# A fourth group of four feature blocks by seven products in the down projection, and the final norm's table loaded in the second half

## The chip, the core and the metric

The kernel runs on one core of one Trainium2 chip. The time is the device time of one execution in microseconds; the kernel before took 1541.56 us (median of 3 runs, 1541.18 to 1541.80).

## What is computed

One layer of a decoder trunk on x of 1 x 256 x 2048 float32: two token mixers, a gated feed-forward part with a causal convolution, and a last RMSNorm. The change touches the last projection of the feed-forward part and the norm behind it:

```python
    h = rmsnorm(x, norm_ffn_w[l])
    gate, up = jnp.split(jnp.einsum('bsd,df->bsf', h, w_up[l]), 2, axis=-1)
    gate = causal_dwconv(gate, conv_ffn_w[l]) + conv_ffn_b[l]
    x = x + jnp.einsum('bsf,fd->bsd', jax.nn.gelu(gate, approximate=False) * up, w_down[l])
return rmsnorm(x, norm_final_w)
```

Here S = 256 tokens, D = 2048 and d_ff = 5632, so w_down is 5632 x 2048.

## The kernel before

**Numbers in two parts.** A float32 operand is kept as two float32r parts: a high part (whi, hhi), made by a cast on ACT (L289), and a low part (wlo, hlo), the difference, made by a subtraction on DVE (L297; called a split below). A product of two operands is three matmuls: high by high, low by high, high by low (`products`, L1356). One matmul takes 128 features of 128 tokens against 128 x 512 of a weight.

**Down projection.** The features are 11 chunks of four blocks of 128 (chunk c: `hhi[c]`, `hlo[c]`); the columns are worked in two halves of 1024, each two tiles of 512. A weight tile is 256 features x 512 columns (0.52 MB). A plain step takes one weight tile against both token halves: 2 x 2 x 3 = 12 matmuls. Four plain steps do a chunk in one column half.

**Seven products.** For the chunks in `SEVEN` a column half is done by Strassen's method in Winograd's form: h of the chunk is a 2 x 2 matrix (token half by feature half), the weights are one (feature half by column tile: parts "11", "12", "21", "22"), and instead of eight products of parts there are seven, of 6 matmuls each (`PRODUCTS`, L152). Products "11", "21" and "T4" take h itself; "T1", "T2", "T3" and "22" take sums of h, which `half_sums` (L1292) makes once a chunk: an addition that puts h together, four sums of 128 x 256 (L1281 to L1284), a cast and a split. On the weights' side T1, T3, T2 and T4 are differences of parts, which DVE forms in place ahead of the cast (L283, tile names quad). The seven results are put together at the end of a half by additions into u and by `plus` (L1573 to L1581, L1504).

**Order.** `stream` (L158) writes the order of the weights of a half: `gaps` gives how many plain steps stand ahead of each group of seven, and behind each product but the first stands one more plain step. With `keeps`, behind the plain steps of the given numbers a weight for the very end is loaded and split early (khi, klo). `begin` (L276) casts and splits two weights ahead of PE's; whi and wlo have three buffers each, the raw loads four. SP issues the raw loads (L209). The 24 parts of the six groups are loaded by POOL's queue (`next_quarter`, L237) into eight places that are handed round (`HOMES`); one is asked for behind each cast of a T product. A scheduler then places the instructions of each engine, in the order that the notation of the fences below shows.

**Around it.** xt and xtl are the residual's tiles (L1555), `weighted` (L1510) multiplies one of their 128 x 512 blocks by the final norm's table nfin, which one transfer of 1 MB on ACT's queue loads ahead of the down projection (L1488) into tile x0. The second half ends with four streamed and four kept weights (`ends`).

Of the kernel before, what the change touches and what calls it, by code (L numbers as in the profile page):

```python
# [35 lines left out]
def kernel(  # L36
# [196 lines left out]
    HOMES = (("xt0", "xt1", "xt2", "xt3"), ("x1a", "x1b", "x2a", "x2b"), ("xt2", "xt3", "x1b", "x1a"),  # L233
             ("x2a", "x2b", "xt3", "xt2"), ("x1b", "x1a", "x2b", "x2a"), ("xt3", "xt2", "x1a", "x1b"))
    asked = [(g, i) for g in range(6) for i in range(4)]

    def next_quarter():  # L237

        if asked:
            g, i = asked.pop(0)  # L240
            half, chunk, what, home = g // 3, SEVEN[g % 3], ORDER[i], HOMES[g][i]
            r = (fp if home[:2] == "xt" else big).tile([P, 2, 512], F32, tag=home, name=nm("quad"))
            nc.gpsimd.dma_start(r, down[2 * half + int(what[1]) - 1][2 * chunk + int(what[0]) - 1])
            quarters[half, chunk, what] = r
# [1047 lines left out]
    def half_sums(c):  # L1292

        if c == SEVEN[2]:
# [152 lines left out]
    for i, step in enumerate(up_steps):  # L1447
# [13 lines left out]
        elif step[0] == "plain":  # L1461
# [6 lines left out]
            if step[1] == NUP - 1 and step[2] == 0:  # L1468
                if step[3] == 5:
                    with tc.issue_after(last_split[0]):  # L1470
                        half_sums(SEVEN[0])
# [15 lines left out]
    nfin = big.tile([P, D], F32, tag="x0", name="nfin")  # L1487
    nc.scalar.dma_start(nfin, norm_final_w.partition_broadcast(P))  # L1488
# [21 lines left out]
    def weighted(t, c):  # L1510
        nc.vector.tensor_tensor(block(t, c), block(t, c), nfin[:, c * 512 : (c + 1) * 512], op=ALU.mult)
# [7 lines left out]
    for hf in range(2):  # L1519
# [11 lines left out]
        for n, step in enumerate(steps[hf]):  # L1531
# [19 lines left out]
            if what == "11" and chunk == SEVEN[1 + hf]:  # L1551
# [4 lines left out]
            if hf == 0 and what == "T2" and chunk != SEVEN[-1]:  # L1556
                with tc.issue_after(last_split[0]):
                    half_sums(SEVEN[SEVEN.index(chunk) + 1])
# [8 lines left out]
            products(ps, high, low, w, alone and what not in began, alone and chunk == SEVEN[-1])  # L1567
            began.add(what)
            if chunk == SEVEN[-1] and what == PRODUCTS[-1]:
# [27 lines left out]
    for t in range(2):  # L1597
        ts = slice(t, t + 1)

        def scaled(c, by, queue):  # L1600
# [5 lines left out]
            else:  # L1606
                nc.vector.scalar_tensor_tensor(xs, xs, rs[:, ts], nfin[:, c * 512 : (c + 1) * 512],
# [70 lines left out]
```

## Time and profile before

| | |
|---|---|
| runs, us | 1541.56 (1541.18 to 1541.80) |
| profiled execution, us | 1542.63 |
| its span, first to last instruction, us | 1540.8 |
| PE busy in the span | 1526.0 us, 99% |
| DVE busy | 1253.4 us, 81% |
| ACT busy | 849.8 us, 55% |
| DMA moved | 310.46 MB, 201 GB/s on average |
| first half of the down projection | about 1299 to 1414 us |
| second half | 1414 to 1533 us; its last split ends at 1516 |

The busy share is an average over stages. In timeline rows the first number is the start in us from the span's start, the second how long the row's instructions took, then engine, line, operation and tiles (written <- read); the last part in brackets is the idle time before it and who ended it. Instructions on PE and DVE overlap at their ends, so what counts for the pace is the distance from start to start, not the length.

### The profile page before, as it was taken

The page shows a single profiled execution, that of the slowest core. Times are in us where ns is not written, and L with a number is a line of the kernel's source. Part 1 is how long each engine was busy: PE and PEld are TensorE (multiplying, and loading weights), DVE is VectorE, ACT ScalarE, POOL GpSimd, SP SyncE. Part 2 cuts the span into 40 slices and gives each one's busy share as a digit, 9 for nine tenths or more (in the row PEclk, how much of TensorE's full clock was granted, in tenths as well). Part 3 has the DMA queues.
Part 4 walks back from the last instruction along what each step waited for, and adds up shares of the span by engine and source line. Part 5 has one row for each costly group of instructions (what it writes and reads, how often), then busy time and mean ns, then how long its engine had stood idle before and what let it go on. Part 6 is the DMA issues. An engine that isn't in the chain of part 4 may idle for free.

```text
span 1540.8 us, 20209 instructions
## 1 busy us (share of the span) xinstructions
PE 1526.0 (99%) x7302; PEld 1257.4 (82%) x7302; DVE 1253.4 (81%) x1776; ACT 849.8 (55%) x1063; POOL 70.8 (5%) x90
## 2 busy tenths in 40 slices
PE   9999999999999999999999999999999999999998
PEld 8887888788878888788888888888788888888886
DVE  6788859896589858987667899999999886878885
ACT  7455446454455445454455676666667665555552
POOL 1010002000100000000000000000000000000100
PEclk9999999999999999999999999999999999999999
DMA  8776757776577766776578646666457467556652
GB/s 276 215 221 199 202 163 214 213 214 183 152 245 205 205 169 201 222 200 186 179 250 300 194 163 217 219 205 205 150 155 242 125 216 267 183 193 205 227 189 90
DMA packets 166674, 310.46 MB, mean 201 GB/s; under 512 B 19458, under 2 KB 23330, under 8 KB 166446
## 3 DMA queue, kind: packets, MB, share of 16 engines
q1 hardware_dynamic: 159456, 287.37, 60.0%
q0 software_dynamic: 5184, 18.88, 3.7%
q10 hardware_dynamic: 1934, 2.93, 0.5%
q8 instruction: 57, 0.93, 0.2%
q14 instruction: 43, 0.35, 0.1%
HBM read 301.75 MB, written 7.38 MB: 201 GB/s over the span
## 4 chain that ended last, share of the span: by engine, by line
PE 92%; DVE 4%; issue 2%; DMA 1%; ACT 0%; POOL 0%; POOLq 0%; DVEq 0%; ACTq 0%
PE psg L1374 25%; PE psm L334 15%; PE psm L332 14%; PE psm L333 14%; PE psm L1359 7%; PE psg L1359 7%; DVE wlo L297 3%; PE psm L1374 2%; PE psm L478 1%; PE psg L377 1%; DVE quad L230 1%; PE psm L1436 1%; DMA vrow<-ev 1%; PE psg L868 1%; DMA mv<-vrow 1%
## 5 line engine op out<-in xcount | busy, mean ns | idle before, releaser
L289 ACT CAST whi<-raw 128x1024 fp32r<-128x1024 f32 x428 | 450.0, 1052 | 428.4 <-PE psm L333 280.2
L297 DVE TENSOR_TENSOR wlo<-raw,whi 128x1024 fp32r<-128x1024 f32 x426 | 517.3, 1220 | 151.2 <-ACT whi L289 146.2
L289 ACT CAST whi<-quad 128x1024 fp32r<-128x1024 f32 x168 | 176.1, 1054 | 141.0 <-DVE quad L230 39.4
L297 DVE TENSOR_TENSOR wlo<-quad,whi 128x1024 fp32r<-128x1024 f32 x168 | 202.6, 1219 | 36.2 <-ACT whi L289 35.3
L334 PE MATMUL psm<-wlo,xhl 128*128 128x512 f32 x432 | 169.5, 393 | 1.6 <-DVE wlo L297 1.6
L332 PE MATMUL psm<-whi,xhl 128*128 128x512 f32 x432 | 169.0, 391 | 0.0
L333 PE MATMUL psm<-whi,xhl 128*128 128x512 f32 x432 | 168.6, 390 | 0.0
L1374 PE MATMUL psg<-whi,fhl 128*128 128x512 f32 x504 | 127.1, 389 | 0.0
L1374 PEld LDWEIGHTS psg<-whi,fhl 128*128 128x128 f32 x504 | 94.4, 188 | 19.5
L334 PEld LDWEIGHTS psm<-wlo,xhl 128*128 128x128 f32 x432 | 81.1, 188 | 19.0 <-DVE wlo L297 2.4
L333 PEld LDWEIGHTS psm<-whi,xhl 128*128 128x128 f32 x432 | 81.1, 188 | 16.8
L332 PEld LDWEIGHTS psm<-whi,xhl 128*128 128x128 f32 x432 | 81.1, 188 | 16.6
L230 DVE TENSOR_TENSOR quad<-quad,quad 128x1024 f32<-128x1024 f32 x72 | 87.6, 1217 | 0.0
L1374 PE MATMUL psg<-wlo,fhl 128*128 128x512 f32 x252 | 69.9, 389 | 0.0
L1374 PE MATMUL psg<-whi,ups 128*128 128x512 f32 x216 | 58.9, 394 | 0.0
L1359 PE MATMUL psm<-whi,hhi 128*128 128x512 f32 (+1 forms) x150 | 58.1, 387 | 0.0
L1359 PE MATMUL psm<-whi,hlo 128*128 128x512 f32 (+1 forms) x150 | 57.9, 386 | 0.0
L1359 PE MATMUL psm<-wlo,hhi 128*128 128x512 f32 (+1 forms) x150 | 57.4, 387 | 0.1
L1374 PEld LDWEIGHTS psg<-wlo,fhl 128*128 128x128 f32 x252 | 47.3, 188 | 9.8
L332 PE MATMUL psm<-whi,mhi 128*128 128x512 f32 x128 | 50.8, 397 | 0.0
L1359 PE MATMUL psg<-whi,hhi 128*128 128x512 f32 (+1 forms) x130 | 50.3, 387 | 0.4 <-ACT whi L289 0.4
L1359 PE MATMUL psg<-whi,hlo 128*128 128x512 f32 (+1 forms) x130 | 50.0, 386 | 0.0
(432 smaller groups left out, 2927.3 us busy)
## 6 DMA issues: line engine op xcount, KB each, us to landing
raw<-in_w_in_dram SPq DMA_DIRECT2D x224, 512.0 KB, 4.2
raw<-in_w_up_dram SPq DMA_DIRECT2D x104, 512.0 KB, 4.8
quad<-in_w_up_dram SPq DMA_DIRECT2D x72, 512.0 KB, 4.9
raw<-in_w_down_dram SPq DMA_DIRECT2D x64, 512.0 KB, 4.7
raw<-in_w_out_dram SPq DMA_DIRECT2D x32, 512.0 KB, 4.2
quad<-in_w_down_dram POOLq DMA_DIRECT2D x24, 512.0 KB, 5.5
mv<-vrow SPq DMA_DIRECT2D x12, 512.0 KB, 4.9
taps<-in_conv_qkv_w_dram SPq DMA_DIRECT2D x16, 256.0 KB, 6.8
```

Of the source, the lines that this page charges most:

```text
L230: nc.vector.tensor_tensor(out_, plus_, minus_, op=ALU.subtract)
L289: nc.scalar.copy(hi, raw)
L297: last_split[0] = nc.vector.tensor_tensor(lo, raw, hi.bitcast(F32), op=ALU.subtract).ins
L332: mm(ps[:, t, :], lh(k, t), hi[:, kk, :], start=(k == 0), stop=False)
L333: mm(ps[:, t, :], ll(k, t), hi[:, kk, :], start=False, stop=False)
L334: mm(ps[:, t, :], lh(k, t), lo[:, kk, :], start=False, stop=(k == nk - 1))
L377: nc.tensor.transpose(pt[:, ff, t * P : (t + 1) * P], src[:, t, f * P : (f + 1) * P], ident)
L478: mm(ps_k0[:, t, :], part(k, t), w[:, kk, :], start=(k == 0 and w is hi and part is xh), stop=(k == KD - 1 and w is lo))
L868: mm(pg0, kq[:, h, 0, 0:P], kq[:, h, :, :], start=True, stop=True)
L1359: mm(ps[:, cs], lhs(kk), part_[:, kk, cs], start=(first and kk == 0 and n == 0), stop=(last and kk == 1 and n == 2), skip_group_check=shared)
L1374: mm(ps, lhs(kk), w[n][:, kk], start=(first and n == 0 and kk == 0 and lhs is high), stop=False, skip_group_check=True)
L1436: nc.tensor.transpose(out_[f // 2][:, f % 2, t * P : (t + 1) * P], e[:, t, f * P : (f + 1) * P], ident)
```

## The change

Chunk 7 joins chunks 8, 9 and 10: in the first half as the fourth group, in the second as the first. A product is now followed by a plain step only behind T1, T3, T2 and "21". The gaps and the keeps change with it. The parts' eight places are handed round by a rule that gives the six old rows and two more. `half_sums` gets places for chunk 7 (tiles y and x0). The norm's table is loaded by POOL's queue in the second half, at product "22" of its second group, into x0, and the four `weighted` of the first half's blocks move from the turn of the halves to product "22" of the last group.

```diff
-    SEVEN = (8, 9, 10)
+    SEVEN = ((8, 9, 10, 7), (7, 8, 9, 10))
     PRODUCTS = ("11", "T1", "22", "T3", "T2", "21", "T4")
-    DIRECT = [c for c in range(KF // 4) if c not in SEVEN]
+    DIRECT = [c for c in range(KF // 4) if c not in SEVEN[0]]
...
-        for n, chunk in zip(gaps, SEVEN):
+        for n, chunk in zip(gaps, SEVEN[half]):
             plain(n)
             for i, what in enumerate(PRODUCTS):
                 steps[half].append(("part", chunk, what))
                 srcs.append((half, chunk, what))
-                if i:
+                if i in (1, 3, 4, 5):
                     plain(1)
         plain(len(todo))
...
-    stream(0, DIRECT, (6, 3, 3))
-    stream(1, DIRECT[:-2], (3, 1, 1), (9, 13, 17, 21))
+    stream(0, DIRECT, (5, 2, 2, 1))
+    stream(1, DIRECT[:-2], (3, 1, 0, 0), (8, 12, 16, 20))
...
-    HOMES = (("xt0", "xt1", "xt2", "xt3"), ("x1a", "x1b", "x2a", "x2b"), ("xt2", "xt3", "x1b", "x1a"),
-             ("x2a", "x2b", "xt3", "xt2"), ("x1b", "x1a", "x2b", "x2a"), ("xt3", "xt2", "x1a", "x1b"))
-    asked = [(g, i) for g in range(6) for i in range(4)]
+    homes = [("xt0", "xt1", "xt2", "xt3"), ("x1a", "x1b", "x2a", "x2b")]
+    while len(homes) < 8:
+        homes.append((homes[-2][2], homes[-2][3], homes[-1][1], homes[-1][0]))
+    asked = [(g, i) for g in range(8) for i in range(4)]
...
-            h = fp.tile([P, 4, S], F32, tag="hlo10" if c == SEVEN[0] else "eu", name=nm("whole"))
+            h = fp.tile([P, 4, S], F32, tag={8: "hlo10", 9: "eu", 7: "y"}[c], name=nm("whole"))
             nc.vector.tensor_tensor(h, hhi[c].bitcast(F32), hlo[c].bitcast(F32), op=ALU.add)
-            b = fp.tile([P, 2, 4, S], F32R, tag="ups", name="sx") if c == SEVEN[0] else \
-                big.tile([P, 2, 4, S], F32R, tag="x3", name="sx")
+            b = fp.tile([P, 2, 4, S], F32R, tag="ups", name="sx") if c == 8 else \
+                big.tile([P, 2, 4, S], F32R, tag="x3" if c == 9 else "x0", name="sx")
...
-    nfin = big.tile([P, D], F32, tag="x0", name="nfin")
-    nc.scalar.dma_start(nfin, norm_final_w.partition_broadcast(P))
+    nfin = []
...
+            if hf and what == "22" and chunk == SEVEN[hf][1]:
+                nfin.append(big.tile([P, D], F32, tag="x0", name="nfin"))
+                nc.gpsimd.dma_start(nfin[0], norm_final_w.partition_broadcast(P))
+            if hf and what == "22" and chunk == SEVEN[hf][3]:
+                for c in range(2):
+                    for t in range(2):
+                        with tc.issue_after(last_split[0]):
+                            weighted(t, c)
-            if what == "11" and chunk == SEVEN[1 + hf]:
+            if what == "11" and chunk == (SEVEN[0][1], SEVEN[1][3])[hf]:
...
                 for t in range(2):
                     plus(t, c, own[c, t])
                     squared(t, c, c)
-                    weighted(t, c)
```

How the instructions move is shown at three places, all on DVE, whose rows PE waits for. In a row, wlo<-quad is the split of a product's weights, wlo<-raw that of a plain step's, quad<-quad a subtraction of parts, klo a kept weight's split; sums, whole and sx belong to `half_sums`, y and hlo10 to the last feature chunk's elementwise work, x1024 is the length of a row of 128 partitions. The lines of the changed kernel are one higher.

The first is the start of the first group of the first half, before:

```order
L297 TENSOR_TENSOR wlo_2019_11297<-raw_2017_11293,whi_2018_11295 128x1024
L1344 TENSOR_TENSOR y_2008_11227<-psg_2012_11259,y_2008_11227 128x512
L1344 TENSOR_TENSOR y_2008_11227<-psg_2013_11264,y_2008_11227 128x512
L297 TENSOR_TENSOR wlo_2021_11313<-quad_1966_10999,whi_2020_11311 128x1024
L1352 TENSOR_TENSOR hlo10_11272<-y_2008_11227,hhi10_11271 128x1024
L283 TENSOR_TENSOR quad_1966_10999<-quad_1972_11035,quad_1966_10999 128x1024
L283 TENSOR_TENSOR quad_1972_11035<-quad_1979_11073,quad_1972_11035 128x1024
L297 TENSOR_TENSOR wlo_2023_11330<-quad_1966_10999,whi_2022_11328 128x1024
L297 TENSOR_TENSOR wlo_2027_11350<-raw_2025_11346,whi_2026_11348 128x1024
```

and in the change:

```order
L298 TENSOR_TENSOR wlo_2018_11293<-quad_1966_10999,whi_2017_11291 128x1024
L1345 TENSOR_TENSOR y_2008_11225<-psg_2012_11257,y_2008_11225 128x512
L1345 TENSOR_TENSOR y_2008_11225<-psg_2013_11262,y_2008_11225 128x512
L284 TENSOR_TENSOR quad_1966_10999<-quad_1972_11035,quad_1966_10999 128x1024
L1353 TENSOR_TENSOR hlo10_11270<-y_2008_11225,hhi10_11269 128x1024
L284 TENSOR_TENSOR quad_1972_11035<-quad_1979_11073,quad_1972_11035 128x1024
L298 TENSOR_TENSOR wlo_2020_11310<-quad_1966_10999,whi_2019_11308 128x1024
L298 TENSOR_TENSOR wlo_2024_11330<-raw_2022_11326,whi_2023_11328 128x1024
```

The split of product "11" takes the place of the sixth plain step's, ahead of the multiplications of y; from it to T1's split (wlo_2020) the rest is the same work.

The second is the way into the last group of the first half, which was chunk 10's, before:

```order
L283 TENSOR_TENSOR quad_2058_11495<-quad_2058_11495,quad_2043_11424 128x1024
L1282 TENSOR_TENSOR sums_2100_11716<-sums_2100_11716,y_2008_11227 128x256
L1284 TENSOR_TENSOR sums_2100_11716<-y_2008_11227,sums_2100_11716 128x256
L297 TENSOR_TENSOR wlo_2105_11750<-quad_2058_11495,whi_2104_11748 128x1024
L297 TENSOR_TENSOR wlo_2109_11764<-raw_2107_11760,whi_2108_11762 128x1024
L1286 TENSOR_TENSOR sh_2099_11715<-sums_2100_11716,sh_2098_11714 128x1024
L297 TENSOR_TENSOR wlo_2112_11782<-raw_2110_11778,whi_2111_11780 128x1024
L297 TENSOR_TENSOR wlo_2115_11794<-raw_2113_11790,whi_2114_11792 128x1024
L297 TENSOR_TENSOR wlo_2118_11812<-raw_2116_11808,whi_2117_11810 128x1024
L297 TENSOR_TENSOR wlo_2120_11828<-quad_2075_11590,whi_2119_11826 128x1024
L283 TENSOR_TENSOR quad_2075_11590<-quad_2086_11653,quad_2075_11590 128x1024
```

and is chunk 7's in the change, from T4's subtraction of the group ahead (the split of its "21", the addition for chunk 7's h and a plain split stand just before):

```order
L284 TENSOR_TENSOR quad_2091_11660<-quad_2091_11660,quad_2077_11592 128x1024
L1282 TENSOR_TENSOR sums_2123_11824<-whole_2122_11821 128x256
L1284 TENSOR_TENSOR sums_2123_11824<-whole_2122_11821 128x256
L1283 TENSOR_TENSOR sums_2123_11824<-sums_2123_11824,whole_2122_11821 128x256
L1285 TENSOR_TENSOR sums_2123_11824<-whole_2122_11821,sums_2123_11824 128x256
L298 TENSOR_TENSOR wlo_2128_11858<-quad_2091_11660,whi_2127_11856 128x1024
L298 TENSOR_TENSOR wlo_2132_11872<-raw_2130_11868,whi_2131_11870 128x1024
L1287 TENSOR_TENSOR sx_11823<-sums_2123_11824,sx_11823 128x1024
L298 TENSOR_TENSOR wlo_2134_11888<-quad_2102_11719,whi_2133_11886 128x1024
L284 TENSOR_TENSOR quad_2102_11719<-quad_2110_11760,quad_2102_11719 128x1024
L284 TENSOR_TENSOR quad_2110_11760<-quad_2116_11791,quad_2110_11760 128x1024
L298 TENSOR_TENSOR wlo_2136_11899<-quad_2102_11719,whi_2135_11897 128x1024
```

Where four plain splits stood between T4's split (wlo_2105) and the next group's first (wlo_2120), one is left, and chunk 7's sums and their split stand among these rows.

The third is the last group of the second half up to T2's split, before:

```order
L297 TENSOR_TENSOR wlo_2279_12634<-raw_2277_12630,whi_2278_12632 128x1024
L1504 SCALAR_TENSOR_TENSOR xtl_12611<-psm_2176_12118,rs_1235_7231,xtl_12611 128x512
L297 TENSOR_TENSOR wlo_2281_12651<-quad_2238_12432,whi_2280_12649 128x1024
L297 TENSOR_TENSOR klo_2292_12710<-raw_2290_12706,khi_2291_12708 128x1024
L297 TENSOR_TENSOR wlo_2284_12663<-raw_2282_12659,whi_2283_12661 128x1024
L297 TENSOR_TENSOR wlo_2286_12680<-quad_2247_12475,whi_2285_12678 128x1024
```

and in the change:

```order
L284 TENSOR_TENSOR quad_2276_12585<-quad_2276_12585,quad_2262_12519 128x1024
L298 TENSOR_TENSOR wlo_2301_12713<-quad_2270_12554,whi_2300_12711 128x1024
L1505 SCALAR_TENSOR_TENSOR xtl_12691<-psm_2184_12132,rs_1235_7231,xtl_12691 128x512
L298 TENSOR_TENSOR wlo_2304_12731<-raw_2302_12727,whi_2303_12729 128x1024
L1512 TENSOR_TENSOR xt0_11536<-xt0_11536,nfin_12412 128x512 x2
L1512 TENSOR_TENSOR xt1_11538<-xt1_11538,nfin_12412 128x512 x2
L298 TENSOR_TENSOR klo_2317_12804<-raw_2315_12800,khi_2316_12802 128x1024
L298 TENSOR_TENSOR wlo_2306_12746<-quad_2276_12585,whi_2305_12744 128x1024
```

Between T3's split (wlo_2301) and T2's (wlo_2306) the four `weighted` are new; the plain step ahead of T3 (wlo_2279) is gone, the one behind it stays.

More of the change, by code (lines that the diff above doesn't have):

```diff
@@ L240, in next_quarter @@
             g, i = asked.pop(0)
-            half, chunk, what, home = g // 3, SEVEN[g % 3], ORDER[i], HOMES[g][i]
+            half, chunk, what, home = g // 4, SEVEN[g // 4][g % 4], ORDER[i], homes[g][i]
             r = (fp if home[:2] == "xt" else big).tile([P, 2, 512], F32, tag=home, name=nm("quad"))
@@ L1292, in half_sums @@
     def half_sums(c):
-        if c == SEVEN[2]:
+        if c == 10:
             h = whole[c]
@@ L1470 @@
                     with tc.issue_after(last_split[0]):
[L1471 removed]
+                        half_sums(SEVEN[0][0])
                 if 4 <= step[3]:
@@ L1510, in weighted @@
     def weighted(t, c):
-        nc.vector.tensor_tensor(block(t, c), block(t, c), nfin[:, c * 512 : (c + 1) * 512], op=ALU.mult)
+        nc.vector.tensor_tensor(block(t, c), block(t, c), nfin[0][:, c * 512 : (c + 1) * 512], op=ALU.mult)
     def direct(ps, kp, t, w, first, last, **more):
@@ L1555 @@
                     nc.gpsimd.dma_start(xts[2 * hf + c], xt_d[:, :, (2 * hf + c) * 512 : (2 * hf + c + 1) * 512])
-            if hf == 0 and what == "T2" and chunk != SEVEN[-1]:
+            if hf == 0 and what == "T2" and chunk != SEVEN[0][-1]:
                 with tc.issue_after(last_split[0]):
-                    half_sums(SEVEN[SEVEN.index(chunk) + 1])
+                    half_sums(SEVEN[0][SEVEN[0].index(chunk) + 1])
             which = OPERAND[what]
@@ L1566 @@
             alone = what in ("11", "T1", "T2", "T3")
-            products(ps, high, low, w, alone and what not in began, alone and chunk == SEVEN[-1])
+            products(ps, high, low, w, alone and what not in began, alone and chunk == SEVEN[hf][-1])
             began.add(what)
-            if chunk == SEVEN[-1] and what == PRODUCTS[-1]:
+            if chunk == SEVEN[hf][-1] and what == PRODUCTS[-1]:
                 c0, c1 = 2 * hf, 2 * hf + 1
@@ L1606, in scaled @@
             else:
-                nc.vector.scalar_tensor_tensor(xs, xs, rs[:, ts], nfin[:, c * 512 : (c + 1) * 512],
+                nc.vector.scalar_tensor_tensor(xs, xs, rs[:, ts], nfin[0][:, c * 512 : (c + 1) * 512],
                                                op0=ALU.mult, op1=ALU.mult)
```

## The prediction

> **What bounds the kernel now.** I read the windows first: one row for each column half of the down projection, with the busy time of PE, PE's weight loads, DVE, ACT and POOL, the granted clock, DMA's share and GB/s. Then who waited on PE's side, the chain of waits, and PE's timeline where it stood.
>
> ```profile
> 1299.00:1414.00 115.00, 114.87 (x516) 94.95 (x515) 92.71 (x94) 60.22 (x63) 8.67 (x12) 1.00 0.58 192
> 1414.00:1517.00 103.00, 102.62 (x453) 84.65 (x452) 85.65 (x80) 56.64 (x61) 5.77 (x8) 1.00 0.58 192
> PEld psg L1359 <- ACT whi L289: 0.8, 1, 0.8
> PEld psm L1359 <- DVE wlo L297: 0.6, 1, 0.6
> 1332.09 19.04 PE psm L1359 x84
> 1444.55 0.39 PE L1359 MATMUL psg<-whi,hlo 128*128 128x512 f32 x1
> 1445.32 0.50 PE L1359 MATMUL psg<-whi,hhi 128*128 128x512 f32 x1 [0.38 <-ACT whi L289]
> 1445.66 0.39 PE L1359 MATMUL psg<-whi,hlo 128*128 128x512 f32 x1
> ```
>
> PE bounds both halves: it is idle 0.13 + 0.38 us in 218, and stood at two places only. The chain's 84 matmuls in 19.04 us give its pitch, 0.227 us, so a plain step (12 matmuls) is 2.72 us and a product (6) is 1.36 us. A stop costs its length plus 0.11 for starting again (1445.32 to 1445.66 instead of 0.227). DVE is the next to watch: 178.4 of 218 us busy, 40 us of room.
>
> **What is saved.** A group of four blocks in one column half was 4 plain steps, 48 matmuls; it becomes 7 products, 42. Two groups: 12 matmuls x 0.227 = **-2.72 us** on the path.
>
> **What is added.** Per group three more weights to cast (ACT) and split (DVE), and four subtractions (DVE); once, the sums of h for chunk 7. The prices:
>
> ```profile
> 1347.04 1.22 DVE L297 TENSOR_TENSOR wlo<-quad,whi 128x1024 fp32r<-128x1024 f32 x1 [1.95 <-ACT whi L289]
> 1348.30 2.49 DVE L283 TENSOR_TENSOR quad<-quad,quad 128x1024 f32<-128x1024 f32 x2
> 1350.72 1.22 DVE L297 TENSOR_TENSOR wlo<-quad,whi 128x1024 fp32r<-128x1024 f32 x1
> 1337.64 1.22 DVE L297 TENSOR_TENSOR wlo<-quad,whi 128x1024 fp32r<-128x1024 f32 x1
> 1338.78 1.22 DVE L297 TENSOR_TENSOR wlo<-raw,whi 128x1024 fp32r<-128x1024 f32 x1
> 1336.18 0.42 DVE L1281 TENSOR_TENSOR sums<-whole 128x256 f32<-128x256 f32 x1
> 1336.51 0.42 DVE L1283 TENSOR_TENSOR sums<-whole 128x256 f32<-128x256 f32 x1
> 1417.67 0.74 DVE L1504 SCALAR_TENSOR_TENSOR xt<-psm,rs,xt 128x512 f32<-128x512 f32 x1
> 1418.33 0.68 DVE L1511 TENSOR_TENSOR xt<-xt,nfin 128x512 f32<-128x512 f32 x1
> 1418.93 0.74 DVE L1504 SCALAR_TENSOR_TENSOR xt<-psm,rs,xt 128x512 f32<-128x512 f32 x1
> 1379.95 1.05 ACT L289 CAST whi<-quad 128x1024 fp32r<-128x1024 f32 x1 [2.12 <-PE psm L1359]
> ```
>
> From start to start DVE pays 1.14 us for a split or subtraction (1337.64 to 1338.78), 1.26 where it touches what the row ahead wrote or read (1347.04 to 1348.30), 0.33 for one of the four sums, 0.66 for a `plus`, 0.60 for a `weighted`. So DVE gets 2 x 7 x 1.14 + 2 x 1.14 + 4 x 0.33 = 19.6 us more, half of its 40 us of room. On average that hides; it does not locally. With four plain steps to seven products a group lasts 7 x 1.36 + 4 x 2.72 = 20.4 us on PE and takes 15 x 1.14 = 17.1 us of DVE (20.7 in the first half, with the next chunk's sums); before it was 25.8 and 19.4 (23.0). And DVE cannot work ahead: three weight buffers, so a cast waits for PE to end the weight three back (1379.95, released by PE). I therefore walked DVE's order of the change, row by row at these prices, against PE's pace.
>
> *First group.* Five plain steps lead instead of six, while DVE still has the last feature chunk's elementwise work.
>
> ```profile
> 1309.91 1.23 DVE L297 TENSOR_TENSOR wlo<-raw,whi 128x1024 fp32r<-128x1024 f32 x1 [0.88 <-ACT whi L289]
> 1311.05 1.28 DVE L1344 TENSOR_TENSOR y<-psg,y 128x512 f32<-128x512 f32 x2
> 1312.45 1.05 ACT L1351 CAST hhi<-y 128x1024 fp32r<-128x1024 f32 x1
> 1319.23 0.39 PE L1359 MATMUL psg<-wlo,sx 128*128 128x512 f32 x1
> ```
>
> Now the split of "11" takes the row at 1309.91, the two multiplications follow to 1312.25, then T1's subtraction (1313.39), hlo (after the cast's end, 1313.53), T3's subtraction (1314.67) and T1's split: 1315.81 to 1317.03. PE took that split at 1319.23 before; with one plain step fewer ahead it wants it 2.72 earlier, at 1316.51. Stop 0.5, and the split behind it is late by another 0.3: **0.8**.
>
> *From the third group to chunk 7's, first half.* One plain step between them, and chunk 7's sums on DVE. Count from PE's start of product "21". Its cast is free when the plain step two weights ahead starts T2, 4.08 us before; cast and handover take 1.13, so its split starts at -2.95. Nine rows of 1.14 (that split, the addition for chunk 7's h, a plain split, T4's subtraction and split, a plain split, the sums' split, the split of "11" and T1's subtraction) and the four sums, 1.3, with 0.24 for two dependent rows, end T1's subtraction at 8.9; with the cast T1's high part is there at 10.0. PE is there after three products and two plain steps, 9.52. T1's split, behind T3's subtraction and that cast, ends at 11.3, where PE, with two matmuls of T1 and two of the step behind it done, wants it at 10.9. 0.5 + 0.4, and 0.3 at the split behind it as in the first group: **1.2**.
>
> *Last group, second half.* The four `weighted` (0.60 each) move from the open stretch behind the first half (1418.33) into this group, ahead of a kept split and of T2's. Counted from PE's start of "11", its split starts at -2.95 again; ten rows of 1.14, one `plus` and four `weighted` later, at 11.5, T2's split starts, and ends at 12.7. PE wants it after four products and two plain steps and two matmuls, 11.3: **1.4**.
>
> *Behind it.* From T2's split to T4's DVE has five rows of 1.14, three additions into u (0.60 each), a `plus` and two dependent rows, 8.4, against PE's 8.2: 0.2 late. Then another addition and a `plus`, 1.3 us, stand ahead of the splits of the last streamed weights, where before the group's last plain step and one more gave PE 5.4 us of work; I put 0.7 on that, about half of the 1.3: **0.9** (0 to 1.5).
>
> **At nothing, with bounds.** The kept loads (L172) move; in both orders a kept split stands ahead of T4's subtraction, so I leave the 0.65 us stop at 1445.32 as it is (bounds: gone, -0.65; a transfer as late as the latest below, +2.7). The stop at the turn of the halves (below, 0.3) keeps its work and stays. Casts: seven more of 1.05, the sums' among them, on an ACT with 101 us of room in the two halves. The table's load leaves the up projection's end, where PE was busy all the time (the third row). It now stands on POOL's queue and waits for x0, whose last reader is a product of the group before; the eight parts' loads behind it are asked for a group, some 20 us, ahead of their use, against 5.8 us to land.
>
> ```profile
> 1408.77 0.39 PE L1359 MATMUL psm<-whi,hlo 128*128 128x512 f32 x1
> 1409.29 0.50 PE L1359 MATMUL psm<-wlo,hhi 128*128 128x512 f32 x1
> 1260.00:1300.00 40.00, 40.00 (x186) 33.22 (x185) 29.59 (x36) 23.91 (x28) 4.33 (x6) 1.00 0.86 298
> quad<-in_w_down_dram POOLq DMA_DIRECT2D x18, 512.0 KB, 5.8
> ```
>
> **Sum:** -2.72 + 0.8 + 1.2 + 1.4 + 0.9 + 4 x 0.11 = **+2.0 us**. The profiled execution took 1542.63 (span 1540.8) and would take 1544.6; the median of runs, 1541.56, becomes **1543.6**.
>
> **A rule against it.** POOL issues nine more transfers, 9 x 0.72 us.
>
> ```profile
> 1339.16 0.72 POOL L243 DMA_DIRECT2D quad<-in_w_down_dram  x1 [1.62 <-DVE wlo L297]
> 1339.91 1.22 DVE L1286 TENSOR_TENSOR sx<-sums,sx 128x1024 fp32r<-128x1024 f32 x1
> ```
>
> While POOL issued at 1339.16, DVE's split of 1338.78 and the next row kept their 1.14 pitch. The Trainium skill ("GPSIMD Engine Reference", section "1. Specifications") says that GpSimd's SBUF interface is shared with VectorE, with contention where a DVE instruction has two SBUF inputs. By that rule 6.5 us of DVE time would be lost; by the row none, and the sum goes by the row.
>
> **Rivals.**
>
> 1. *The saving stays.* If DVE slips ahead of my walk by a microsecond at each place, the four stops shrink to nothing and the sum is the saving alone: 1541.56 - 2.72 = 1538.8, at best 1538.2 with the kept stop gone. For it: 20 us of room remain. Against: three buffers keep DVE from using it early. Chance 0.17, nearly all of it within 0.2%.
>
> 2. *Slower: the kept transfers.* ACT casts in order, and a kept cast waits for its transfer with the rest behind it.
>
> ```profile
> 1440.67 1.05 ACT L289 CAST khi<-raw 128x1024 fp32r<-128x1024 f32 x1 [1.21 <-DMA raw<-in_w_down_dram]
> 1472.76 1.05 ACT L289 CAST khi<-raw 128x1024 fp32r<-128x1024 f32 x1 [2.68 <-DMA raw<-in_w_down_dram]
> raw<-in_w_down_dram SPq DMA_DIRECT2D x62, 512.0 KB, 4.7
> ```
>
> The first of these led, through the kept split ahead of T4's subtraction, to the stop at 1445.32; the longer second cost PE nothing, because DVE had idle time to make up. Now DVE has little in a group, and a group moves nine tiles of 0.52 MB in 20.4 us, 231 GB/s, plus the table's and the residual's 2.1 MB over the half's 92 us, 254 GB/s against 192 before. One wait like 2.68 that passes to PE gives +4.7, two +7.4: 1546.2 to 1549. It decides once a kept transfer lands more than 1 us behind its turn. Against: the up projection's end took 298 GB/s without a stop. Chance 0.23.
>
> 3. *Slower: the shared interface.* If POOL's issues do hold DVE, half of 6.5 us falls where DVE is late: 1543.6 + 3.2 = 1546.8. The rows speak against it. Chance 0.05.
>
> My forecast (stops of 3 to 6 us) has 0.55.
>
> **Numbers.** 0.2%, about what a measurement of this kernel can tell from no change, is 3.1 us, so the forecast itself counts as no change. Stops of half my size give -2.72 + 2.4 = 1541.2, of one and a half 1546; reaching to part of both rivals, the range is 1540.2 to 1546.6. Faster by over 0.2% needs rival 1 with the kept stop gone: 0.05. Slower: rivals 2 and 3, 0.27 with the forecast's upper edge. Within: 0.68.
>
> **What would show it.** 12 fewer matmuls of L1360; PE idle in the two halves 4 to 6 us instead of 0.5, at T1 of the first group and of chunk 7's, at T2 of the last group and behind it, released by wlo or whi; DVE busy about 198 us. Wrong if PE's idle time stays below 2 us, if it stands mainly behind khi, or if DVE's rows are longer than 1.22.

## The result, and the profile after

| | before | after |
|---|---|---|
| runs, us: median (lowest to highest) | 1541.66 (1540.14 to 1543.54), 22 runs | 1544.84 (1541.82 to 1545.78), 22 runs |
| ratio, 95% interval | | 1.0018 (1.0011 to 1.0024) |
| profiled execution, us | 1542.63 | 1543.82 |
| its span, us | 1540.8 | 1542.1 |

The ratio makes the change 2.8 us slower, between 1.7 and 3.7 (the medians alone differ by 3.2); the forecast was +2.0, inside 0.2% (3.1 us). The profile's page after, its first part (busy time, share and instructions of each engine), two of its costliest groups and two of its DMA issues:

```profile
PE 1525.7 (99%) x7290; PEld 1254.9 (81%) x7290; DVE 1272.6 (83%) x1796; ACT 856.1 (56%) x1070; POOL 77.2 (5%) x99
...
L298 DVE TENSOR_TENSOR wlo<-raw,whi 128x1024 fp32r<-128x1024 f32 x418 | 508.1, 1221 | 141.5 <-ACT whi L290 137.0
L298 DVE TENSOR_TENSOR wlo<-quad,whi 128x1024 fp32r<-128x1024 f32 x182 | 219.9, 1221 | 30.4 <-ACT whi L290 27.3
...
raw<-in_w_down_dram SPq DMA_DIRECT2D x56, 512.0 KB, 5.4
...
quad<-in_w_down_dram POOLq DMA_DIRECT2D x32, 512.0 KB, 5.2
```

PE's total is 0.3 us below that of before and DVE's 19.2 us above; a split still takes 1.22 us. From issue to landing the raw loads take 0.7 us more than before (4.7), the parts 0.3 us less (5.5 on the page of before). Over the whole kernel PE reads "99%" in both. What happened is in the two halves, in the windows (columns as in the prediction: stretch, its length, busy time of PE, PEld, DVE, ACT and POOL with their instructions, clock, DMA share, GB/s):

```profile
1297.60:1413.00 115.40, 114.15 (x505) 92.79 (x505) 101.49 (x105) 64.32 (x67) 11.55 (x16) 1.00 0.57 189
1413.00:1518.00 105.00, 103.28 (x452) 83.88 (x451) 95.58 (x90) 59.23 (x64) 9.22 (x13) 1.00 0.61 202
```

957 matmuls instead of 969: twelve fewer, as over the whole kernel (7290 instead of 7302). DVE has 197.1 us instead of 178.4, the clock is 1.00, and PE is idle 1.25 + 1.72 us instead of 0.51. Who ended the waits of PE's matmuls in the halves (engine, tile and line waiting, releaser: us, times, longest; the rows of its weight loads, PEld, are left out):

```profile
PE psg L1360 <- ACT whi L290: 1.1, 2, 0.6
PE psg L1360 <- DVE wlo L298: 0.9, 2, 0.5
PE psm L1360 <- DVE wlo L298: 0.7, 1, 0.7
PE psm L1360 <- ACT whi L290: 0.2, 1, 0.2
```

All are the two parts, high (whi) and low (wlo), of a streamed or a product's weight. PE's timeline shows where (start, length, then what):

```profile
1315.09 0.39 PE L1360 MATMUL psm<-whi,hlo 128*128 128x512 f32 x1
1315.87 0.50 PE L1360 MATMUL psg<-wlo,sx 128*128 128x512 f32 x1 [0.39 <-DVE wlo L298]
...
1389.90 0.39 PE L1360 MATMUL psg<-wlo,hhi 128*128 128x512 f32 x1
1390.93 0.73 PE L1360 MATMUL psg<-whi,sx 128*128 128x512 f32 x2 [0.64 <-ACT whi L290]
1391.88 0.51 PE L1360 MATMUL psm<-whi,hhi 128*128 128x512 f32 x1 [0.22 <-ACT whi L290]
...
1441.82 0.39 PE L1360 MATMUL psg<-whi,hlo 128*128 128x512 f32 x1
1442.75 0.50 PE L1360 MATMUL psg<-wlo,hhi 128*128 128x512 f32 x1 [0.54 <-DVE wlo L298]
...
1501.67 0.39 PE L1360 MATMUL psg<-whi,hlo 128*128 128x512 f32 x1
1502.77 0.50 PE L1360 MATMUL psm<-wlo,sh 128*128 128x512 f32 x1 [0.71 <-DVE wlo L298]
...
1510.61 0.39 PE L1360 MATMUL psg<-whi,hlo 128*128 128x512 f32 x1
1511.03 0.50 PE L1360 MATMUL psg<-wlo,hhi 128*128 128x512 f32 x1
...
1512.29 0.40 PE L1360 MATMUL psg<-whi,hlo 128*128 128x512 f32 x1
1513.13 0.51 PE L1360 MATMUL psg<-whi,hhi 128*128 128x512 f32 x1 [0.44 <-ACT whi L290]
```

A stop is read from start to start here. From 1315.09 to 1315.87 PE took 0.78 us for a matmul that takes 0.227 when nothing is late: 0.55 lost, and the view shows 0.39 of it as idle, because a matmul's row is 0.39 us long while the next starts after 0.227. So the 2.97 us of idle time in the windows stand for more than twice that in lost time. The stop at 1442.75 is the kept weight's of before, at another plain step: in ACT's timeline the kept weight's cast (khi) stands late, and behind it the cast of the plain weight whose split PE then waits for.

```profile
1438.11 1.05 ACT L290 CAST khi<-raw 128x1024 fp32r<-128x1024 f32 x1 [1.38 <-DMA raw<-in_w_down_dram]
1439.06 1.05 ACT L290 CAST whi<-raw 128x1024 fp32r<-128x1024 f32 x1
```

**One measure for all kernels.** The stretch of the down projection, from the start of its first matmul to the start of its last, and in it the lost time: what each distance from start to start has beyond 0.2268 us a matmul (0.1195 where a row is 256 wide), where that is more than 0.02. Ahead of the stretch every kernel but one below does the same work, but for the table's load, which stands there in the kernel before and in no other; yet it starts at 1298.85 us in the profile of before, at 1297.65 in that of after, and anywhere from 1296.3 to 1298.2 in the others. That spread of 2.6 us is as large as the effect; the stretch leaves it out.

| us | before | after | gone or come |
|---|---|---|---|
| stretch | 234.31 | 236.67 | +2.36 |
| lost in it | 1.23 | 6.04 | +4.82 |
| the rest, matmuls at their pace | 233.09 | 230.63 | -2.46 |
| lost at the first group, first half | 0 | 0.87 | +0.87 |
| at T1 of chunk 7's group, first half | 0 | 1.41 | +1.41 |
| at the turn of the halves | 0.40 | 0.55 | +0.15 |
| at the first kept weight | 0.66 | 0.82 | +0.16 |
| at T2 of the last group, second half | 0 | 1.20 | +1.20 |
| behind it | 0 | 1.03 | +1.03 |
| smaller ones | 0.17 | 0.17 | 0 |

Twelve matmuls at 0.2268 are 2.72; the rest fell by 2.46. The other 0.26 is pace: the 960 matmuls of 512 columns that no stop delays take 227.06 ns each instead of 226.77. Most of the slow ones stand right behind a stop, at 0.230 to 0.238 us.

### The profile page after: what moved, and what is told of

The parts are those of the page before. It is cut to its first block, busy times and chain, and to the rows that moved or that the text cites. A ratio compares the mean times of both kernels' runs of the same rounds, so it can differ in the third digit from the quotient of the medians.

```text
span 1542.1 us, 20229 instructions
## 1 busy us (share of the span) xinstructions
PE 1525.7 (99%) x7290; PEld 1254.9 (81%) x7290; DVE 1272.6 (83%) x1796; ACT 856.1 (56%) x1070; POOL 77.2 (5%) x99
## 4 chain that ended last, share of the span: by engine, by line
PE 91%; DVE 5%; issue 2%; DMA 2%; ACT 1%; SPq 0%; POOL 0%; POOLq 0%; DVEq 0%; ACTq 0%
PE psg L1375 25%; PE psm L335 14%; PE psm L333 14%; PE psm L334 14%; PE psm L1360 7%; PE psg L1360 6%; DVE wlo L298 3%; PE psm L1375 2%; PE psm L479 1%; PE psg L378 1%; DVE quad L230 1%; PE psm L1437 1%; PE psg L869 1%; DMA lb<-cdd 1%; ACT whi L290 0%
## 5 line engine op out<-in xcount | busy, mean ns | idle before, releaser
L290 ACT CAST whi<-raw 128x1024 fp32r<-128x1024 f32 x420 | 441.7, 1052 | 424.4 <-PE psm L334 285.4
L298 DVE TENSOR_TENSOR wlo<-raw,whi 128x1024 fp32r<-128x1024 f32 x418 | 508.1, 1221 | 141.5 <-ACT whi L290 137.0
L290 ACT CAST whi<-quad 128x1024 fp32r<-128x1024 f32 x182 | 190.7, 1053 | 140.0 <-DVE quad L230 38.0
L298 DVE TENSOR_TENSOR wlo<-quad,whi 128x1024 fp32r<-128x1024 f32 x182 | 219.9, 1221 | 30.4 <-ACT whi L290 27.3
L1360 PE MATMUL psm<-whi,hhi 128*128 128x512 f32 (+1 forms) x140 | 54.4, 388 | 0.2 <-ACT whi L290 0.2
L1360 PE MATMUL psm<-whi,hlo 128*128 128x512 f32 (+1 forms) x140 | 54.1, 386 | 0.0
L1360 PE MATMUL psm<-wlo,hhi 128*128 128x512 f32 (+1 forms) x140 | 53.6, 388 | 0.0
L244 POOL DMA_DIRECT2D quad<-in_w_down_dram x32 | 23.1, 723 | 586.9 <-DVE wlo L298 487.9
L335 PE MATMUL psm<-wlo,mhi 128*128 128x512 f32 x128 | 50.0, 390 | 0.0
```

The source lines that it names most:

```text
L290: nc.scalar.copy(hi, raw)
L298: last_split[0] = nc.vector.tensor_tensor(lo, raw, hi.bitcast(F32), op=ALU.subtract).ins
L335: mm(ps[:, t, :], lh(k, t), lo[:, kk, :], start=False, stop=(k == nk - 1))
L1360: mm(ps[:, cs], lhs(kk), part_[:, kk, cs], start=(first and kk == 0 and n == 0), stop=(last and kk == 1 and n == 2), skip_group_check=shared)
```

## The experiments

The main theory, A, is the prediction's: the saving of 2.72 us is real, and DVE's rows come too late at four places, each for a cause of its own. Its rivals are that one common cause holds DVE or its inputs: POOL's transfer issues (theory B), or the kept weights' transfers (theory C). Sizes are stretches from one profile, ratios are of the runs.

**The four `weighted` behind the last split.** They leave the last group of the second half.

```diff
-            if hf and what == "22" and chunk == SEVEN[hf][3]:
-                for c in range(2):
-                    for t in range(2):
-                        with tc.issue_after(last_split[0]):
-                            weighted(t, c)
...
     ws += wk
+    for t in range(2):
+        for c in range(2):
+            with tc.issue_after(last_split[0]):
+                weighted(t, c)
```

> The change, with the four multiplications by the table (weighted, first half's blocks) placed behind the last split instead of inside the last group. Theory A (DVE's queue is late at four places, one of them because of these four rows): the stops at T2 of the last group (1.2 us in the change) and behind it (1.2 us) go, the others stay (0.9 at T1 of the first group, 1.4 at T1 of chunk 7, 0.5 at the turn, 0.8 at the kept split); the stretch from the first product step to the last matmul falls from 236.7 to 234.2 us, the time about 2.5 us below the change, equal to the kernel before within 0.5. Theory B (POOL's extra issues hold DVE at a shared interface): POOL issues the same, so the stretch stays at 236.7. Theory C (kept transfers are late): the same 236.7.

Measured: stretch 234.47; ratio 1.0002 (0.9993 to 1.0011). DVE's timeline of the changed kernel ahead of T2's split, and then that of this one:

```profile
1496.82 1.21 DVE L298 TENSOR_TENSOR wlo<-raw,whi 128x1024 fp32r<-128x1024 f32 x1
1497.96 2.49 DVE L1512 TENSOR_TENSOR xt<-xt,nfin 128x512 f32<-128x512 f32 x4
1500.37 1.22 DVE L298 TENSOR_TENSOR klo<-raw,khi 128x1024 fp32r<-128x1024 f32 x1
1501.50 1.22 DVE L298 TENSOR_TENSOR wlo<-quad,whi 128x1024 fp32r<-128x1024 f32 x1
```

```profile
1497.50 1.22 DVE L298 TENSOR_TENSOR wlo<-raw,whi 128x1024 fp32r<-128x1024 f32 x1
1498.63 1.22 DVE L298 TENSOR_TENSOR klo<-raw,khi 128x1024 fp32r<-128x1024 f32 x1
1499.77 1.22 DVE L298 TENSOR_TENSOR wlo<-quad,whi 128x1024 fp32r<-128x1024 f32 x1
```

From the streamed split to T2's it is 4.68 us with the `weighted` (1496.82 to 1501.50), 2.27 without. Both stops of the last group, 1.20 and 1.03, are gone, and the other stops stand nearly as they were (0.87, 1.41, 0.90): moving the four `weighted` alone takes 2.2 us off. The scheduler also put T4's subtraction one row earlier here, so how much is the rows' own time and how much the order behind T2 is not separated.

**One plain step moved ahead of chunk 7's group.**

```diff
-    stream(0, DIRECT, (5, 2, 2, 1))
+    stream(0, DIRECT, (5, 2, 1, 2))
```

> The change, with one plain step of the first half moved from behind the last group to ahead of it... that is from the third gap to the fourth: gaps (5, 2, 1, 2) instead of (5, 2, 2, 1). The amount of work is the same on every engine. Theory A: two plain steps give DVE 1.6 us more room ahead of chunk 7's T1, so that stop (1.4 us) goes, and the one fewer ahead of chunk 10 costs less than 0.3; stretch 235.3 instead of 236.7, time 1.4 below the change. Theories B and C: no effect, 236.7.

Measured: stretch 235.60; ratio 1.0010 (1.0001 to 1.0019). The stop of 1.41 at T1 is gone and none of its size takes its place (0.22 appears at chunk 10's group, which gave up the step, and the kept weight's stop is 0.92 instead of 0.82). That splits the change further: 1.1 us of it is where one plain step stands.

**The table's move alone.** The kernel before, in which only the table's load and the four `weighted` go where the change puts them.

```diff
-    nfin = big.tile([P, D], F32, tag="x0", name="nfin")
-    nc.scalar.dma_start(nfin, norm_final_w.partition_broadcast(P))
+    nfin = []
...
+            if hf and what == "22" and chunk == SEVEN[0]:
+                nfin.append(big.tile([P, D], F32, tag="x0", name="nfin"))
+                nc.gpsimd.dma_start(nfin[0], norm_final_w.partition_broadcast(P))
+            if hf and what == "22" and chunk == SEVEN[2]:
+                for c in range(2):
+                    for t in range(2):
+                        with tc.issue_after(last_split[0]):
+                            weighted(t, c)
...
-                    weighted(t, c)
```

> The kernel before (three groups, its old gaps and keeps) with only the table's move: loaded by POOL's queue in the second half at product 22 of its first group, the four weighted at product 22 of the last group. Theory A: 2.4 us of DVE land in the last group, where even with six plain steps DVE has too little room; stops of 1.5 to 2 us in the last group and behind it, stretch 235.8 to 236.3 against 234.3, time 1.5 to 2 above the kernel before. Theory B (the group's POOL issues are to blame): one issue more, no effect, 234.3. Theory C: the table's 1 MB makes a kept transfer late: a stop before 1465 us and none in the last group.

Measured: stretch 237.50; ratio 1.0016 (1.0007 to 1.0025). More than expected. 0.73 and 1.41 are lost in the last group, about the 2 us expected there; 0.76 more at a place that neither kernel had, where ACT's timeline and then PE's show:

```profile
1455.36 1.05 ACT L289 CAST khi<-raw 128x1024 fp32r<-128x1024 f32 x1 [2.47 <-DMA raw<-in_w_down_dram]
```

```profile
1457.03 0.39 PE L1359 MATMUL psg<-wlo,hhi 128*128 128x512 f32 x1
1457.42 0.74 PE L1359 MATMUL psg<-whi,sx 128*128 128x512 f32 x2
```

A kept transfer came 2.47 us behind its turn, the casts behind it were late, and 0.76 of it reached PE at the next product. So the second rival of the prediction does happen, in a kernel with less to do on DVE than the change. And the table's part of the change is by itself as dear (+3.2) as the whole change (+2.4).

**Chunk 7 without sums of its own.** Its products take chunk 10's sums, so the kernel leaves out an addition, four sums, a cast and a split.

```diff
+        if c == 7:
+            sums_of[c] = sums_of[10]
+            return
```

> The change without chunk 7's own sums: its products take the sums of chunk 10, so 3.6 us of DVE (an addition, four sums, a split) and one cast are left out. Theory A: DVE is 3.6 us earlier at T1 of chunk 7 and its stop of 1.4 us goes whole, the others stay to 0.1; stretch 235.2 to 235.4 instead of 236.7. Theory B (POOL's issues): the issues are all there, the stop stays, 236.7. Theory C (late transfers): the same, 236.7.

Measured: stretch 236.16, one run of 1542.91 us. The stop at T1 fell from 1.41 to 0.24, as expected; but the stretch is 0.5 shorter only, because the kept weight's stop rose from 0.82 to 1.50 (ACT's timeline has its cast 2.07 us behind its turn instead of 1.38):

```profile
1437.26 1.05 ACT L290 CAST khi<-raw 128x1024 fp32r<-128x1024 f32 x1 [2.07 <-DMA raw<-in_w_down_dram]
```

This fits a simple reading, which no run isolates: a stop that is taken away brings the work behind it forward against a transfer that doesn't come sooner.

**Twice as many issues on POOL: a first try.** A small load with no reader behind each part's.

```diff
             nc.gpsimd.dma_start(r, down[2 * half + int(what[1]) - 1][2 * chunk + int(what[0]) - 1])
+            nc.gpsimd.dma_start(scratch, down[0][0][:, :, 0:8])
```

> The change with a second, small transfer issued by POOL ahead of the entry of each of the 32 parts (256 pieces of 32 bytes, into a tile that nothing reads), so POOL issues about 32 times 0.7 us more. Theory A: the same four stops, stretch 236.7 within 0.4, DVE's splits at 1.22 us on average. Theory B: if nine more issues cost the stretch 2 us, 32 more cost it 5 or more, 241 us and above, and DVE's rows get longer. Theory C: a little more DMA work, at most a later kept transfer, below 1 us.

Measured: ratio 1.0121 (1.0107 to 1.0135). Nothing ties the extra loads to their place, and the scheduler set them at the start of the kernel, where POOL's timeline has one every few us, each waiting for the one before to land:

```profile
12.34 0.72 POOL L246 DMA_DIRECT2D scratch<-in_w_down_dram  x1 [5.05 <-DMA scratch<-in_w_down_dram]
17.84 0.72 POOL L246 DMA_DIRECT2D scratch<-in_w_down_dram  x1 [4.78 <-DMA scratch<-in_w_down_dram]
```

The down projection starts 16 us later than before; which work of the early stages was held was not followed up. Its stretch is 238.13, above the 236.7 expected: the four stops are those of the change, and 2.2 us are lost at the first kept weight instead of 0.82. With no extra issue in the halves, the kernel does not test what it was made for.

**Twice as many issues on POOL, in their place.** The small load now fills the first columns of the part's own tile, so it cannot move away.

```diff
-            nc.gpsimd.dma_start(r, down[2 * half + int(what[1]) - 1][2 * chunk + int(what[0]) - 1])
+            part_ = down[2 * half + int(what[1]) - 1][2 * chunk + int(what[0]) - 1]
+            nc.gpsimd.dma_start(r[:, :, 0:8], part_[:, :, 0:8])
+            nc.gpsimd.dma_start(r, part_)
```

> The change with every part loaded twice over: ahead of each of the 32 loads on POOL's queue stands a second one, of the first 8 columns of the same part into the same tile, so that POOL issues 32 more transfers in the stage itself, about 27 of them within the two halves, at 0.72 us each. Nothing else moves, and DVE's and ACT's rows stand nearly as before. Theory A (POOL's issues do not hold DVE): DVE's rows stay at 1.22 us, the four stops stay at 0.87, 1.41, 1.20 and 1.03, and the stretch of the down projection is 236.7, at most 0.8 more where a part lands later. Theory B (they hold DVE through the shared interface): each issue costs DVE up to 0.72 us, half of it where DVE is late, which gives the stretch 241 or more and DVE rows above 1.22 beside the issues.

Measured: stretch 237.37; ratio 1.0020 (1.0011 to 1.0029). The groups of POOL's issues between 1290 and 1530 us (xcount, busy us, mean ns, idle before), and then DVE's groups in the halves:

```profile
L246 POOL DMA_DIRECT2D quad<-in_w_down_dram x27 | 19.5, 723 | 55.3 <-DMA quad<-in_w_down_dram 54.9 <-issue 0.3
L245 POOL DMA_DIRECT2D quad<-in_w_down_dram x26 | 18.7, 720 | 72.1 <-DVE wlo L300 27.0 <-DVE quad L286 25.9 <-DVE sums L1284 7.5
```

```profile
L300 DVE TENSOR_TENSOR wlo<-quad,whi 128x1024 fp32r<-128x1024 f32 x56 | 68.2, 1222 | 13.6 <-ACT whi L292 11.4 <-PE psg L1362 1.3 <-PE psm L1362 0.6
L300 DVE TENSOR_TENSOR wlo<-raw,whi 128x1024 fp32r<-128x1024 f32 x49 | 59.7, 1221 | 6.9 <-ACT whi L292 4.4 <-PE psg L380 2.2
L286 DVE TENSOR_TENSOR quad<-quad,quad 128x1024 f32<-128x1024 f32 x32 | 39.1, 1223 | 0.7
```

POOL issues 53 transfers there instead of 26, and DVE's splits and subtractions take what they took; the four stops are 0.87, 1.40, 1.22 and 1.02. The 0.7 us more are three other stops (0.34, 0.22 and 0.87) while the stop at the first kept weight is gone. They are not parts that came late: in the halves no subtraction and no cast waited for a part's transfer. The scheduler set DVE's rows around the kept splits in another order here, so "nothing else moves" does not hold; what made the three stops was not followed further. Theory B falls: the rows and the four stops are those of the change.

**The first kept weight one plain step later, nothing else.**

```diff
-    stream(1, DIRECT[:-2], (3, 1, 0, 0), (8, 12, 16, 20))
+    stream(1, DIRECT[:-2], (3, 1, 0, 0), (9, 12, 16, 20))
```

> The change with the first kept weight behind the 9th plain step of the second half instead of the 8th, and nothing else. Theory A (the late first kept transfer is one cause by itself): the kept stop of 0.82 goes or falls below 0.3, the four stops of late splits stay at 0.87, 1.41, 1.20 and 1.03 within 0.2, and the stretch is 235.8 against 236.67. Rival (the kept transfers are what makes DVE late further on): the stops at 205 and 213 fall too, and the stretch is 234 or less. Rival 2 (the transfers of the group are late wherever the kept weight stands): the stop of 0.8 only moves, and the stretch stays at 236.7.

Measured: stretch 235.82; ratio 1.0006 (0.9996 to 1.0016). The stop of 0.82 is gone, and the four others are 0.88, 1.39, 1.18 and 1.01: the kept transfer is a cause by itself, and not what makes DVE late further on. Theory C falls as the common cause. On ACT and DVE it looks like this, ACT's row ahead of DVE's:

```profile
1439.61 1.05 ACT L290 CAST khi<-raw 128x1024 fp32r<-128x1024 f32 x1 [1.24 <-DMA raw<-in_w_down_dram]
```

```profile
1440.69 1.23 DVE L298 TENSOR_TENSOR klo<-raw,khi 128x1024 fp32r<-128x1024 f32 x1 [0.94 <-ACT khi L290]
```

The transfer is late by 1.24 us here too, but the subtraction for T4 now stands ahead of the kept split, and the wait falls into time that DVE had.

**The stops taken away one after another.** Three kernels, each the one before it and one thing more. The first is the change with the `weighted` moved as above and the gaps of the second experiment.

```diff
-    stream(0, DIRECT, (5, 2, 2, 1))
+    stream(0, DIRECT, (5, 2, 1, 2))
...
     ws += wk
+    for t in range(2):
+        for c in range(2):
+            with tc.issue_after(last_split[0]):
+                weighted(t, c)
```

> The change with weighted behind the last split and gaps (5, 2, 1, 2). Theory A: the two gains add: left are 0.9 at T1 of the first group, 0.5 at the turn, 0.8 at the kept split; stretch 232.7, that is 1.6 us below the kernel before and 4.0 below the change, time about 1540. Theories B and C: no better than the change.

Measured: stretch 233.57; ratio 0.9992 (0.9983 to 1.0001). 0.9 above the expectation; 0.33 us is the kept weight's stop again, 1.15 instead of 0.82, and two small ones, 0.22 together, stand in the first half; the rest was not taken apart. The second kernel has the first kept weight one plain step later as well.

```diff
-    stream(1, DIRECT[:-2], (3, 1, 0, 0), (8, 12, 16, 20))
+    stream(1, DIRECT[:-2], (3, 1, 0, 0), (9, 12, 16, 20))
```

> The kernel of the run called both, with the first kept weight loaded behind the ninth plain step of the second half instead of the eighth, so that its split no longer stands ahead of T4's subtraction in DVE's order. Theory A with C in this one place: the stop at 144 us of the stretch (1.15 in both, 0.8 in the change) goes, stretch 232.4 instead of 233.6. If that stop were of DVE's general shortage and not of the kept transfer's lateness, it would appear a step later with about the same size, 233.6.

Measured: stretch 232.42; ratio 0.9988 (0.9979 to 0.9997): as expected, and the kept weight's stop is gone. The third changes the first group of the first half, where DVE still has the last chunk's elementwise work: its plain steps stand behind "11", "22", T2 and "21" instead of T1, T3, T2 and "21".

```diff
-                if i in (1, 3, 4, 5):
+                if i in ((0, 2, 4, 5) if half == 0 and chunk == 8 else (1, 3, 4, 5)):
```

> The kernel of kept_later with the plain steps of the first group of the first half standing behind 11, 22, T2 and 21 instead of T1, T3, T2 and 21: the plain step behind 11 gives PE 2.7 us of work while DVE finishes the last chunk's elementwise rows. Theory A: the stop at T1 of the first group (0.9) goes too and only the one at the turn of the halves (0.55) is left; stretch 231.3 to 231.6, 2.7 to 3.0 below the kernel before, time about 1538.8, so the whole saving of the twelve matmuls arrives. If the fourth group costs anything but these stops, the stretch stays above 232.4.

Measured: stretch 231.59, median 1538.08 (1536.01 to 1539.53), ratio 0.9979 (0.9970 to 0.9988): 3.2 us faster than before, between 1.8 and 4.6, and faster than the change. The two halves of this kernel in the windows:

```profile
1296.30:1412.00 115.70, 115.69 (x515) 94.72 (x514) 103.32 (x107) 63.72 (x67) 11.56 (x16) 1.00 0.58 194
1412.00:1514.00 102.00, 102.00 (x453) 84.40 (x453) 93.67 (x87) 59.36 (x64) 9.22 (x13) 1.00 0.61 203
```

PE is idle 0.01 us of 217.7 (from start to start 1.01 us are lost, 0.55 of them at the turn of the halves), with DVE as busy as in the change (203.6 us over the whole stretch against 204.1). The same work on the same engines, 5 us shorter, by the order alone.

## Why the prediction was right

Forecast 1543.6 (+2.0), measured +2.8 (1.7 to 3.7), in the stretch +2.36. By its steps:

- *The saving.* 12 x 0.227 = 2.72. Measured: 2.46, the stretch without its lost time; the pace gives back 0.26. In the last kernel above, with about as much lost time as before (1.01 against 1.23), nearly all of it comes through: the stretch is 234.31 - 231.59 = 2.72 shorter, 0.22 of that being lost time.
- *Four stops on late splits.* Right in place, and DVE is what ends last at the first group, at chunk 7's T1 and at T2. With their four restarts they were put at 4.7; measured 4.51. That this is so close is partly luck: each place has two stops and two restarts, so eight restarts (0.89) stand in for four (0.44), and the stops themselves are 3.62 instead of 4.3. First group: 0.8 and 0.11, measured 0.87. In DVE's timeline T1's split starts at 1314.59; the walk had it at 1315.81 in the times of before, which is 1314.61 when the stage's earlier start (1.20) is taken off. Chunk 7's T1: 1.2 and 0.11, measured 1.41. T2 of the last group: 1.4 and 0.11, measured 1.20. Behind it: 0.9 and 0.11, measured 1.03. The 0.2 at T4's split came as walked (0.19). The 0.7, half of a bound, was the weakest term; its number held (0.61 and a restart), its reason did not: at 1513.13 PE waits for a cast, not for a split behind an addition and a `plus`, and that cast had waited 1.03 us for PE to be done with an older weight (below, 1512.03).

DVE's timeline of the changed kernel has that split of the first group, and the walk at chunk 7's group row by row; ACT's, behind it, has the casts that PE waited for at chunk 7's T1 and at the end:

```profile
1314.59 1.22 DVE L298 TENSOR_TENSOR wlo<-quad,whi 128x1024 fp32r<-128x1024 f32 x1
...
1382.37 0.42 DVE L1282 TENSOR_TENSOR sums<-whole 128x256 f32<-128x256 f32 x1
...
1383.83 1.22 DVE L298 TENSOR_TENSOR wlo<-quad,whi 128x1024 fp32r<-128x1024 f32 x1
1384.97 1.22 DVE L298 TENSOR_TENSOR wlo<-raw,whi 128x1024 fp32r<-128x1024 f32 x1
1386.10 1.22 DVE L1287 TENSOR_TENSOR sx<-sums,sx 128x1024 fp32r<-128x1024 f32 x1
1387.24 1.22 DVE L298 TENSOR_TENSOR wlo<-quad,whi 128x1024 fp32r<-128x1024 f32 x1
1388.49 2.48 DVE L284 TENSOR_TENSOR quad<-quad,quad 128x1024 f32<-128x1024 f32 x2
1390.91 1.23 DVE L298 TENSOR_TENSOR wlo<-quad,whi 128x1024 fp32r<-128x1024 f32 x1
```

```profile
1389.83 1.05 ACT L290 CAST whi<-quad 128x1024 fp32r<-128x1024 f32 x1 [3.37 <-DVE quad L284]
1390.78 1.04 ACT L290 CAST whi<-raw 128x1024 fp32r<-128x1024 f32 x1
...
1512.03 1.05 ACT L290 CAST whi<-raw 128x1024 fp32r<-128x1024 f32 x1 [1.03 <-PE psg L1360]
```

At chunk 7's group the rows follow each other without a gap, at 1.14 us and at 1.25 where a row needs the one ahead, four sums in 1.46 (1382.37 to 1383.83; put at 1.3): DVE is the engine that ends last here, though it is busy 88% of this half (101.49 of 115.40). What passes its lateness on is ACT: T1's cast waits for T1's subtraction, and the plain weight's cast stands behind T1's. PE waits for these two casts, longer than put for the first (0.80 instead of 0.5). T1's split, on which the walk put another 0.4, ends at 1392.14, ahead of its first matmul at 1392.45.

Of the other steps:

- *DVE's load.* 19.6 us more, 198 in all; measured 18.7 more (197.07 against 178.36).
- *At nothing.* The kept weight's stop was left at 0.65 and measured 0.82: its transfer came 1.38 us behind its turn instead of 1.21, about the 0.16 added. The turn of the halves, said to keep its work and stay, grew by 0.15, and the pace behind the stops took 0.26; why the turn grew stays open. These three, 0.57 together, are the term that the sum mis-sized; less 0.2 that the four stops were below theirs, it is the whole difference between +2.0 and +2.36. What the table's load costs apart from its readers was not tried.
- *Rival 1, the saving stays.* Not in the change. The reason given against it, that DVE cannot work ahead, is only half the story: the last kernel above has the same buffers and the same DVE work, and no stop above 0.21 us but at the turn. What it needed was an order that gives each urgent row slack.
- *Rival 2, the kept transfers.* The late transfer is real (1.38 us) but reached PE at one place, for 0.16 more than before. The other three kept casts waited for their transfers 0, 0.33 and 0 us, where they had waited 0.84, 2.68 and 0 before, and the second half's window shows 202 GB/s where the rival was worked out with 254. That it can do more is shown by the run with the table alone (0.76 at a second place) and that without chunk 7's sums (1.50).
- *Rival 3, the shared interface.* By the run with twice the issues, 53 of 0.72 us leave DVE's rows at 1.22. The Trainium skill ("GPSIMD Engine Reference", section "1. Specifications") says that GpSimd and VectorE contend for a shared SBUF interface where a DVE instruction has two SBUF inputs; the trace shows none for issuing transfers, which is all that POOL does here beside two tiny additions. Work of POOL on data was not tried.
- *What would show it.* The places, the releasers, twelve fewer matmuls and the 1.22 us rows came as said. The idle time did not: 4 to 6 us were forecast for the windows and 2.97 stood there. The stops were counted from start to start and then looked for in a view that hides part of each; as lost time they are 6.0.

## What to carry to other kernels

When work moves from the busiest engine to the next one, averages (here 40 us of room for 20 us of work) say little: walk the second engine's queue in order, at its start-to-start prices, from the last point where it is tied to the first engine, and look for rows without a reader in a hurry that stand ahead of one with such a reader. Follow a late row through the engine that reads it, since the wait that ends last may stand there. Then place those rows, and the first engine's spare work, so that each urgent row has slack: here four moves of order turned +2.8 us into -3.2. And measure a stage from its own first to its own last instruction when the kernel around it varies by as much as the effect.

## What the runs showed beside

- Work ahead of the stage that was unchanged but for the table's load ended anywhere in a window of 2.6 us, from one profile to the next, at clocks between 0.998 and 0.999.
- A stop has a tail: after each one the next matmul takes 0.34 us to hand over instead of 0.227, whether PE had waited 0.39 or 0.71 us (1315.87 to 1316.20, 1502.77 to 1503.11), and a few behind that one 0.230 to 0.238.
- 32 tiny loads with no reader on POOL's queue cost 18 us (1559.73 against 1541.47) where they were free to move; with 32 tied to their place in the down projection its stretch was 0.7 us longer.
